# Attention rows: the inverse sums of grouped-query rows move to GpSimd, the high parts of the values to ScalarE

## The chip, the core and the metric

The kernel runs on one core of one Trainium2 chip. The metric is the device time of one execution in microseconds (us), the median of three runs. Five engines work from queues of their own, each strictly in order: TensorE (PE; its weight loads are listed as PEld), VectorE (DVE), ScalarE (ACT), GpSimd (POOL) and SyncE (SP), which issues all DMAs here.

## The reference, cut to what matters

One layer of a diffusion backbone over 2048 latent tokens and 256 context tokens, width 1024. After a modulated RMS norm, one wide projection feeds three parallel mixers (pooling, differential attention, grouped-query attention), each multiplied by a gate path; they are merged and projected out. The change touches the two attentions:

```
def _diff_core(q, k, v, lam):
    s = jnp.einsum('bqhcd,bkhcd->bhcqk', q, k).astype(jnp.float32) * (DIFF_HEAD_DIM ** -0.5)
    p = jax.nn.softmax(s, axis=-1)
    a = (p[:, :, 0] - lam * p[:, :, 1]).astype(v.dtype)
    return jnp.einsum('bhqk,bkhe->bqhe', a, v)

def _gqa_core(q, k, v):
    s = jnp.einsum('bqgrd,bkgd->bgrqk', q, k).astype(jnp.float32) * (GQA_HEAD_DIM ** -0.5)
    p = jax.nn.softmax(s, axis=-1).astype(v.dtype)
    return jnp.einsum('bgrqk,bkgd->bqgrd', p, v)
```

Each of 128 queries by 2304 keys is one *row* below: 4 differential heads with two softmaxes each, 8 grouped-query heads over 2 key/value heads, 16 blocks of 128 queries. That makes 128 differential and 128 grouped-query rows.

## The kernel before

Products keep float32-like accuracy by splitting operands into a high and a low float16 part. There are three stages: projections (to about 565 us of the span), attention (565 to about 2370 us), merge and output projection (to the end).

**A turn of the attention loop.** The loop runs over 256 rows in a fixed order that repeats every four: two differential rows of one query block (called d0 and d1 here), then two grouped-query rows (g0 and g1). Turn i does this for row i (`score_row`, L804 to L822):

- PE: ten matmuls into two PSUM tiles, `sa` (1024 columns) and `sb` (1280 columns). Both have one buffer, so the scores of a row can start only when ScalarE has read the `sa` of the row before.
- DVE: the maximum of `sa` (L815), of `sb` (L816), and the scaled maximum (L817).
- ACT: exponentials of `sa` (L820) and `sb` (L821) into `pt`, each with its sum into column 2 or 3 of the small tile `nm`.

The normalisation lags behind. Two turns later ACT writes `hi`, the float16 of `pt` times the inverse sum (L898, L874), and DVE writes `lo`, the remainder (L903, L879). For a differential row DVE first combines the two softmaxes (L870). SP transposes `hi` and `lo` by DMA into `th`, from which PE forms the products with the values. PE fills the rest of a turn with these products (L917, L943) and with *gate units*, matmuls of another projection that hang on nothing in the attention. So PE always has work beside the scores, but its order is fixed: if the scores wait, what stands behind them waits too.

**Where the inverse sum stands.** `inverse_sum` is two DVE instructions of one column each: add the two sums and scale (L825), reciprocal (L827). For a grouped-query row it is issued first in the turn in which `hi` is made, ahead of the maxima of that turn's row on DVE.

**Where the values are split.** When a head begins, its values are loaded in six parts (`vr`) and split into high and low (`vt`) over three turns, two parts per turn (`load_values`, L787 to L802): a multiply (L798) and a multiply-subtract (L800) for each part, all on DVE, behind L817 of the turn and ahead of its `lo` or combine. There are six such heads (four differential, 128 columns a part of 3 tiles; two grouped-query, 64 columns), so 36 parts in 18 turns.

**Order.** Each engine executes in the order in which the program is written. GpSimd in this stage splits the weight columns of the gate units (`col_split`: L159, L163, L165, twice each for a column, some 36 columns) and squares the differential outputs (L927).

The lines that decide the rest:

```
        for i in range(NR + 7):
            ...
            todo, split_later = split_later, []
            for f in ahead.pop(i, ()):
                f()
            ...
            if i < NR:
                kind, h, j, o, c = rows[i]
                ...
            for f in todo + after.pop(i, []):
                f()
```

`ahead` holds `hi`, `todo` the value splits, `after` the combine and `lo`.

Of the kernel before, what the change touches and what calls it, by code (L numbers as in the profile page):

```python
# [12 lines left out]
F32 = mybir.dt.float32  # L13
F32R = mybir.dt.float32r
I32 = mybir.dt.int32
AF = mybir.ActivationFunctionType
ALU = mybir.AluOpType
# [4 lines left out]
P = 128  # L22
# [10 lines left out]
PSC = 4096.0  # L33
# [24 lines left out]
def block_kernel(ctx: ExitStack, tc, x, xT, ctxt, cc, ada_w, ada_bT, norm_gT, w_qkv, w_gate, gains,  # L58
                 rope_row, rope_col, lam, sublnT, pool_w, pool_scaleT, pool_edge, w_br, w_out, out,
                 dbg=None, stop=9):  # L60
    nc = tc.nc
# [28 lines left out]
    vscale = cst.tile([P, 2], F32, name="vscale")  # L90
# [121 lines left out]
    with tc.tile_pool(name="p1", bufs=1) as sp, tc.tile_pool(name="p1s", bufs=1, space=PSUM) as pp:  # L212
# [460 lines left out]
        for n, kind in enumerate(QKV_ORDER):  # L673
# [12 lines left out]
            for t in range(first, NT):  # L686
                u = t - first
                g, i = divmod(t, 3)
# [67 lines left out]
    with tc.tile_pool(name="p2", bufs=1) as sp, tc.tile_pool(name="p2s", bufs=1, space=PSUM) as pp:  # L756
# [4 lines left out]
        for n in range(32):  # L761
            for o in range(2):
                rows += [("d", n // 8, n % 8, o, c) for c in range(2)]
                m = 2 * n + o
                rows += [("g", m // 8, m % 8, p, 0) for p in range(2)]
        NR = len(rows)
        ahead = {}
# [3 lines left out]
        def at(table, slot, f):  # L771
            table.setdefault(max(slot, 0), []).append(f)
# [10 lines left out]
                    in_=qD[pair][:, half * 64:(half + 1) * 64, j * 256:(j + 1) * 256].rearrange("s p t -> p s t"))  # L783

        VC = 3

        def load_values(key, src, c0, n, m, part):  # L787

            if part == 0:

                use_up((key[0], key[1] - 1))
                values[key] = sp.tile([P, NKT, 2, n], F16, name="vt", tag="vt" + key[0], bufs=1 if key[0] == "d" else 2)
            vt = values[key][:, part * VC:(part + 1) * VC]
            vr = sp.tile([P, VC, n], F32, name="vr", tag="vr", bufs=2)
            dma(out=vr, in_=src[part * VC:(part + 1) * VC, :, c0:c0 + n].rearrange("k p d -> p k d"))

            def split():
                nc.vector.tensor_scalar(out=vt[:, :, 0, :], in0=vr, scalar1=vscale[:, m:m + 1], scalar2=None,  # L798
                                        op0=ALU.mult)
                nc.vector.scalar_tensor_tensor(out=vt[:, :, 1, :], in0=vr, scalar=vscale[:, m:m + 1],  # L800
                                               in1=vt[:, :, 0, :], op0=ALU.mult, op1=ALU.subtract)
            return split  # L802

        def score_row(i, qt, kt, o, m):  # L804

            sa = pp.tile([P, SA], F32, name="sa", tag="sa", bufs=1)
            sb = pp.tile([P, SB], F32, name="sb", tag="sb", bufs=1)
            for k0 in range(0, NTOK, 512):
                k1 = min(k0 + 512, NTOK)
                dst = sa[:, k0:k1] if k0 < SA else sb[:, k0 - SA:k1 - SA]  # L810
                for s in range(2):
                    nc.tensor.matmul(dst, lhsT=qt[:, s, o * P:(o + 1) * P], rhs=kt[:, k0:k1], start=(s == 0),  # L812
                                     stop=(s == 1))
            nm = sp.tile([P, 4], F32, name="nm", tag="nm", bufs=8)
            nc.vector.tensor_reduce(out=nm[:, 0:1], in_=sa, axis=AX.X, op=ALU.max, negate=True)  # L815
            nc.vector.tensor_reduce(out=nm[:, 1:2], in_=sb, axis=AX.X, op=ALU.max, negate=True)  # L816
            nc.vector.tensor_scalar(out=nm[:, 0:1], in0=nm[:, 0:1], scalar1=nm[:, 1:2], scalar2=escale[:, m:m + 1],  # L817
                                    op0=ALU.min, op1=ALU.mult)
            pt = sp.tile([P, NTOK], F32, name="pt", tag="pt", bufs=4)
            nc.scalar.activation(out=pt[:, :SA], in_=sa, func=AF.Exp, scale=escale[:, m:m + 1], bias=nm[:, 0:1], accum_out=nm[:, 2:3])  # L820
            nc.scalar.activation(out=pt[:, SA:], in_=sb, func=AF.Exp, scale=escale[:, m:m + 1], bias=nm[:, 0:1], accum_out=nm[:, 3:4])  # L821
            return pt, nm  # L822

        def inverse_sum(nm, scale):
            nc.vector.tensor_scalar(out=nm[:, 2:3], in0=nm[:, 2:3], scalar1=nm[:, 3:4], scalar2=scale, op0=ALU.add,  # L825
                                    op1=ALU.mult)
            nc.vector.reciprocal(out=nm[:, 3:4], in_=nm[:, 2:3])  # L827

        def part(name):
            return sp.tile([P, NTOK], F16, name=name, tag="parts", bufs=4)  # L830
# [6 lines left out]
        def use_up(key):  # L837
            while any(k == key for k, _ in avs):
                finish_first()

        def turn(src, step, a, o):
            if o == 0:
                while a == 0 and len(live) == 2:

                    finish_first()
                if a == 0:
                    live.append(step)
                turned.setdefault(step, []).append(sp.tile([P, NKT, 256], F16, name="th", tag="turned", bufs=4))
            nc.sync.dma_start_transpose(out=turned[step][a][:, :, o * P:(o + 1) * P], in_=src)
# [3 lines left out]
        def diff_row(i, h, j, o, c):  # L853
            pt, nm = score_row(i, queries[h, j, c], keys[h, c], o, 0)
            if c == 0:
                first[0] = pt, nm
                at(ahead, i + 1, lambda: inverse_sum(nm, lscale[:, 0:1]))
                return
# [4 lines left out]
            def ratio():  # L863

                inverse_sum(nm, lscale[:, 0:1])
                nc.vector.tensor_scalar(out=nm[:, 2:3], in0=nm[:, 3:4], scalar1=n0[:, 2:3], scalar2=neglam[:, 0:1],
                                        op0=ALU.mult, op1=ALU.mult)
# [22 lines left out]
        def gqa_row(i, h, j, o):  # L890
            pt, nm = score_row(i, queries[4 + h, j, 0], keys["g", h // 4], o, 1)
            step = (4 + h, j)
            box = {}

            def high():
                inverse_sum(nm, 1.0 / PSC)
                box["hi"] = part("hi")
                nc.scalar.activation(out=box["hi"], in_=pt, func=AF.Copy, scale=nm[:, 3:4])  # L898
                turn(box["hi"], step, 0, o)

            def low():
                lo = part("lo")
                nc.vector.scalar_tensor_tensor(out=lo, in0=pt, scalar=nm[:, 3:4], in1=box["hi"], op0=ALU.mult,  # L903
                                               op1=ALU.subtract)
                turn(lo, step, 1, o)

            at(ahead, i + 2, high)
            at(after, i + 2, low)
            if o == 1:
                at(fills, i + 4, lambda: (("g", h // 4), gqa_av(h, j, values["g", h // 4], turned.pop(step))))  # L910
# [27 lines left out]
        def gqa_av(h, j, vt, pts):  # L938
            ps = acc("av")
            n = 0  # L940
            for a in range(2):
                for k in range(NKT):
                    nc.tensor.matmul(ps[:, :256], lhsT=vt[:, k, :, :].rearrange("p a d -> p (a d)"),  # L943
                                     rhs=pts[a][:, k, :], start=(n == 0), stop=(n == 2 * NKT - 1))
                    n += 1
                    yield 0.107
            live.remove((4 + h, j))
            r0 = (h % 2) * 64
            ot = sp.tile([P, 256], F32, name="ot", tag="ot", bufs=2)
            sh = sp.tile([64, 256], F32, name="sh", tag="o2", bufs=2)  # L950
            nc.scalar.activation(out=sh, in_=ps[64:128, :256], func=AF.Copy, scale=oscale[64:128, 1:2])
            nc.vector.scalar_tensor_tensor(out=ot[r0:r0 + 64, :], in0=ps[0:64, :256], scalar=oscale[0:64, 1:2], in1=sh,
                                           op0=ALU.mult, op1=ALU.add)
            dma(out=oD[4 + h // 2][r0:r0 + 64, j * 256:(j + 1) * 256], in_=ot[r0:r0 + 64, :])
# [40 lines left out]
        for i in range(NR + 7):  # L995
            row_now[0] = i
            on_act[0] = i >= NR - 2
            avs += [f() for f in fills.pop(i, ())]
            todo, split_later = split_later, []
            for f in ahead.pop(i, ()):  # L1000
                f()
            if i == 0:
                run_gates(HEAD_UNITS - 2)
            if i < NR:
                kind, h, j, o, c = rows[i]
                if kind == "d":
                    diff_row(i, h, j, o, c)
                else:
                    gqa_row(i, h, j, o)
                spent[0] += 1.95  # L1010
            for f in todo + after.pop(i, []):
                f()
            goal = total * (i + 1) / NR if i < NR else spent[0] + 24 * 0.2135 * (i < NR + 4)
            while avs and spent[0] < goal:
                t = next(avs[0][1], None)
                if t is None:
                    avs.pop(0)
                else:
                    spent[0] += t
            while spent[0] < goal:  # L1020
                t = next(dense, None)
                if t is None:
                    break
                spent[0] += t
# [321 lines left out]
```

## Time and profile before

| | |
|---|---|
| median of 3 runs | 2906.23 us (2905.7 to 2908.32) |
| the profiled execution | 2909.97 us, of which span 2908.2 us |
| PE busy | 2787.0 us (96%) |
| DVE busy | 2222.6 us (76%) |
| ACT busy | 1623.7 us (56%) |
| POOL busy | 699.2 us (24%) |

PE is busy nearly throughout, so the profile is read by PE's idle time: where it stands, and what ended it. The shares of the other engines say little by themselves; in the attention stage DVE's is far above its mean. The mean granted TensorE clock is 0.987 of full speed, and 1.00 in most of the attention stage.

### The profile page before, as it was taken

Reading aid. Unit: us, or ns where it says so; the run is one execution under the profiler, and the core shown is the slowest. Engines: PE = TensorE matmul, PEld = TensorE weight load, DVE = VectorE, ACT = ScalarE, POOL = GpSimd, SP = SyncE. Lnnn points to the kernel's source line nnn. Section 1 sums busy time; section 2 is a strip of 40 time slices with the busy share of each in tenths; the row PEclk is TensorE's granted clock in tenths of the full one; section 3 lists DMA queues with packets and bytes.
Section 4 is the critical chain, followed back from the end, with each engine's and each line's share of the span. In section 5 each row is a group of like instructions: output and inputs, shape, how many; then the busy total and the mean of one; then the engine's idle time right before and its main releaser. Section 6 shows DMA issues by size and latency. Waiting matters only on the chain. (4 is left out here: it accounts for less than half of the span.)

```text
span 2908.2 us, 41087 instructions
## 1 busy us (share of the span) xinstructions
PE 2787.0 (96%) x15031; PEld 1653.7 (57%) x15031; DVE 2222.6 (76%) x2829; ACT 1623.7 (56%) x2168; POOL 699.2 (24%) x699
## 2 busy tenths in 40 slices
PE   7999999999999999999989999999999997999999
PEld 2544435655555555555545555555555555787787
DVE  4547657498888898888889888899988856756753
ACT  3844432266766666767756777676776743222221
POOL 1035645411111112110212011202111114443431
PEclk8999999999999999999999999999999998999999
DMA  7345552378888888889798998998987977767674
GB/s 255 109 124 158 138 161 60 104 167 174 184 168 169 178 182 174 167 178 183 161 198 183 180 184 180 176 195 182 185 180 169 184 144 245 238 224 256 208 247 154
DMA packets 1134266, 516.46 MB, mean 178 GB/s; under 512 B 985040, under 2 KB 1038704, under 8 KB 1134064
## 3 DMA queue, kind: packets, MB, share of 16 engines
q1 hardware_dynamic: 1134064, 513.84, 75.2%
q8 instruction: 118, 1.93, 0.3%
q14 instruction: 84, 0.69, 0.1%
HBM read 208.24 MB, written 78.97 MB: 99 GB/s over the span
## 5 line engine op out<-in xcount | busy, mean ns | idle before, releaser
L179 PE MATMUL gate<-hT,gws 128*128 128x512 f16 x3840 | 869.2, 380 | 0.5 <-ACT gt L185 0.5
L179 PEld LDWEIGHTS <-gws 128*128 128x128 f16 x3840 | 373.4, 98 | 419.2 <-issue 17.8
L820 ACT ACTIVATE pt<-sa,nm,escale 128x1024 f32<-128x1024 f32 x256 | 308.3, 1204 | 448.4 <-DVE nm L817 400.2
L812 PEld LDWEIGHTS <-qt 128*128 128x128 f16 x2560 | 249.9, 98 | 356.9 <-issue 72.7
L532 PE MATMUL qkv<-wt,hT 128*128 128x512 f16 (+1 forms) x1920 | 397.3, 362 | 0.0
L816 DVE TENSOR_REDUCE nm<-sb 128x1 f32<-128x1280 f32 x256 | 379.1, 1481 | 0.6 <-PE sb L812 0.6
L815 DVE TENSOR_REDUCE nm<-sa 128x1 f32<-128x1024 f32 x256 | 311.4, 1216 | 71.3 <-PE sa L812 62.2
L821 ACT ACTIVATE pt<-sb,nm,escale 128x1280 f32<-128x1280 f32 x256 | 360.3, 1407 | 0.0
L903 DVE SCALAR_TENSOR_TENSOR lo<-pt,nm,hi 128x2304 f16<-128x2304 f32 x128 | 338.5, 2645 | 6.4 <-ACT hi L898 4.7
L812 PE MATMUL sb<-kt,qt 128*128 128x512 f16 (+1 forms) x1536 | 319.5, 344 | 20.4 <-ACT pt L821 19.3
L898 ACT ACTIVATE hi<-pt,nm 128x2304 f16<-128x2304 f32 x128 | 283.3, 2213 | 95.6 <-issue 44.8
L532 PEld LDWEIGHTS <-hT 128*128 128x128 f16 x1920 | 189.7, 99 | 176.8 <-issue 11.3
L812 PE MATMUL sa<-kt,qt 128*128 128x512 f16 x1024 | 263.0, 379 | 21.7 <-ACT pt L820 17.3
L943 PE MATMUL av<-th,vt 128*128 128x256 f16 x2304 | 266.0, 274 | 13.9 <-DMA th<-hi 7.4
L1190 PE MATMUL br<-bt,wt 128*128 128x512 f32 x1152 | 267.7, 393 | 1.6 <-DVE wt L1045 1.6
L943 PEld LDWEIGHTS <-vt 128*128 128x128 f16 x2304 | 226.2, 98 | 44.7 <-issue 12.8
L1190 PEld LDWEIGHTS br<-bt,wt 128*128 128x128 f32 x1152 | 217.3, 189 | 50.6 <-DVE wt L1045 2.7
L927 POOL TENSOR_TENSOR o<-ot 128x256 f32<-128x256 f32 x32 | 19.7, 614 | 861.4 <-ACT ot L923 861.4
L163 POOL TENSOR_SCALAR gws<-gw 128x512 f16<-128x512 f32 x74 | 68.2, 922 | 597.7 <-PE gate L179 593.8
L917 PE MATMUL av<-th,vt 128*128 128x256 f16 x1728 | 198.9, 273 | 0.0
L1222 PE MATMUL out<-y,wt 128*128 128x512 f32 x768 | 185.0, 399 | 11.6 <-DVE wt L1045 4.9
L917 PEld LDWEIGHTS <-vt 128*128 128x128 f16 x1728 | 169.0, 98 | 19.9
(207 smaller groups left out, 3156.3 us busy)
## 6 DMA issues: line engine op xcount, KB each, us to landing
tD<-gt SPq DMA_DIRECT2D x96, 256.0 KB
wr<-in_w_br SPq DMA_DIRECT2D x32, 768.0 KB
ld<-tD SPq DMA_DIRECT2D x96, 256.0 KB
scan<-in_w_gate SPq DMA_DIRECT2D x40, 512.0 KB
gw<-in_w_gate SPq DMA_DIRECT2D x80, 256.0 KB
qt<-qD SPq DMA_DIRECT2D x256, 64.0 KB
wr<-in_w_out SPq DMA_DIRECT2D x32, 512.0 KB
sgD<-gt SPq DMA_DIRECT2D x48, 256.0 KB
```

Source lines behind the costliest of these rows:

```text
L179: nc.tensor.matmul(ps, lhsT=w[:, b, k, :], rhs=hT[k][:, a, c * CH:(c + 1) * CH], start=(n == 0), stop=(n == 3 * KT - 1))
L532: nc.tensor.matmul(ps[:, :width], lhsT=tokens_of(t, k, a), rhs=wt[k][:, b, :width], start=(n == 0), stop=(n == 3 * KT - 1))
L812: nc.tensor.matmul(dst, lhsT=qt[:, s, o * P:(o + 1) * P], rhs=kt[:, k0:k1], start=(s == 0), stop=(s == 1))
L815: nc.vector.tensor_reduce(out=nm[:, 0:1], in_=sa, axis=AX.X, op=ALU.max, negate=True)
L816: nc.vector.tensor_reduce(out=nm[:, 1:2], in_=sb, axis=AX.X, op=ALU.max, negate=True)
L820: nc.scalar.activation(out=pt[:, :SA], in_=sa, func=AF.Exp, scale=escale[:, m:m + 1], bias=nm[:, 0:1], accum_out=nm[:, 2:3])
L821: nc.scalar.activation(out=pt[:, SA:], in_=sb, func=AF.Exp, scale=escale[:, m:m + 1], bias=nm[:, 0:1], accum_out=nm[:, 3:4])
L898: nc.scalar.activation(out=box["hi"], in_=pt, func=AF.Copy, scale=nm[:, 3:4])
L903: nc.vector.scalar_tensor_tensor(out=lo, in0=pt, scalar=nm[:, 3:4], in1=box["hi"], op0=ALU.mult, op1=ALU.subtract)
L917: nc.tensor.matmul(ps[:, :256], lhsT=vt[:, k, v, :], rhs=pts[a][:, k, :], start=(n == 0), stop=(n == 3 * NKT - 1))
L943: nc.tensor.matmul(ps[:, :256], lhsT=vt[:, k, :, :].rearrange("p a d -> p (a d)"), rhs=pts[a][:, k, :], start=(n == 0), stop=(n == 2 * NKT ...
L1190: nc.tensor.matmul(ps, lhsT=wb[:, a, 4 * br + k, :], rhs=branch_tile(c, br, k)[:, b], start=(m == 0), stop=(m == 11))
```

## The change

Three edits in the attention stage.

1. The values' high part is made by an ACT activation (copy with a scale) in place of a DVE multiply. The low part stays on DVE and reads the high part.
2. For grouped-query rows the two one-column instructions go to GpSimd: add and scale, and a power with exponent -1 in place of the reciprocal. For differential rows they stay on DVE.
3. These two are issued one turn after the row, ahead of the scores of that turn, not in the turn in which `hi` uses them.

```
+        mone = sp.tile([P, 1], F32, name="mone")
+        nc.vector.memset(mone, -1.0)
...
             def split():
-                nc.vector.tensor_scalar(out=vt[:, :, 0, :], in0=vr, scalar1=vscale[:, m:m + 1], scalar2=None,
-                                        op0=ALU.mult)
+                nc.scalar.activation(out=vt[:, :, 0, :], in_=vr, func=AF.Copy, scale=vscale[:, m:m + 1])
                 nc.vector.scalar_tensor_tensor(out=vt[:, :, 1, :], in0=vr, scalar=vscale[:, m:m + 1],
                                                in1=vt[:, :, 0, :], op0=ALU.mult, op1=ALU.subtract)
...
+        def inverse_beside(nm):
+
+            nc.gpsimd.tensor_scalar(out=nm[:, 2:3], in0=nm[:, 2:3], scalar1=nm[:, 3:4], scalar2=1.0 / PSC, op0=ALU.add,
+                                    op1=ALU.mult)
+            nc.gpsimd.tensor_tensor(out=nm[:, 3:4], in0=nm[:, 2:3], in1=mone, op=ALU.pow)
...
             def high():
-                inverse_sum(nm, 1.0 / PSC)
                 box["hi"] = part("hi")
                 nc.scalar.activation(out=box["hi"], in_=pt, func=AF.Copy, scale=nm[:, 3:4])
                 turn(box["hi"], step, 0, o)
...
+            at(ahead, i + 1, lambda: inverse_beside(nm))
             at(ahead, i + 2, high)
             at(after, i + 2, low)
```

The lines of the changed kernel lie up to seven further down: L815 becomes L816, L821 becomes L822, L903 becomes L909, and so on.

VectorE before, at the second of the three turns in which the second differential head's values are split (`vr` are the loaded values, `vt` the split ones, `nm` the small tile of maxima and sums):

```order
L825 TENSOR_SCALAR nm<-nm 128x1
L827 RECIPROCAL nm<-nm 128x1
L825 TENSOR_SCALAR nm<-nm,lscale 128x1
L827 RECIPROCAL nm<-nm 128x1
L815 TENSOR_REDUCE nm<-sa 128x1
L816 TENSOR_REDUCE nm<-sb 128x1
L817 TENSOR_SCALAR nm<-nm,escale 128x1
L798 TENSOR_SCALAR vt<-vr,vscale 128x3x128
L800 SCALAR_TENSOR_TENSOR vt<-vr,vscale,vt 128x3x128
L798 TENSOR_SCALAR vt<-vr,vscale 128x3x128
L800 SCALAR_TENSOR_TENSOR vt<-vr,vscale,vt 128x3x128
L903 SCALAR_TENSOR_TENSOR lo<-pt,nm,hi 128x2304
```

The same place on VectorE in the changed kernel:

```order
L826 TENSOR_SCALAR nm<-nm,lscale 128x1
L828 RECIPROCAL nm<-nm 128x1
L816 TENSOR_REDUCE nm<-sa 128x1
L817 TENSOR_REDUCE nm<-sb 128x1
L818 TENSOR_SCALAR nm<-nm,escale 128x1
L801 SCALAR_TENSOR_TENSOR vt<-vr,vscale,vt 128x3x128 x2
L909 SCALAR_TENSOR_TENSOR lo<-pt,nm,hi 128x2304
```

The first inverse sum and the two multiplies are gone; the two multiply-subtracts stand directly behind the scaled maximum.

ScalarE in the changed kernel, the same turn (the exponentials of `sa` and `sb`, then the two copies, then a gate unit's eviction):

```order
L904 ACTIVATE hi<-pt,nm 128x2304
L821 ACTIVATE pt,nm<-sa,nm,escale 128x1024
L822 ACTIVATE pt,nm<-sb,nm,escale 128x1280
L800 ACTIVATE vt<-vr,vscale 128x3x128 x2
L188 ACTIVATE gt<-gate,ginv 128x512
```

Before, the eviction stood directly behind the two exponentials; the two copies have come between them.

GpSimd in the changed kernel, from the end of one column split to the start of the next (`gw` and `gws` are a weight column, `o_6436` is a squared output):

```order
L165 TENSOR_TENSOR gws<-gw,gws 128x512 x2
L832 TENSOR_SCALAR nm<-nm 128x1
L834 TENSOR_TENSOR nm<-nm,mone 128x1
L832 TENSOR_SCALAR nm<-nm 128x1
L834 TENSOR_TENSOR nm<-nm,mone 128x1
L934 TENSOR_TENSOR o_6436<-ot 128x256
L159 TENSOR_SCALAR gw<-gw,gws 128x512
```

Before, L927 (now L934) followed directly on L165. Now the inverse sums of two grouped-query rows stand between them, behind the whole column split.

## Rows read from the trace of the kernel before

**Rows 1.** Busy time by stretch of the attention stage: stretch, length, engines, clock, DMA.
```profile
564.00:632.00 68.00, 63.61 (x311) 30.53 (x310) 60.57 (x80) 40.69 (x51) 8.78 (x10) 0.97 0.78 176
632.00:1054.00 422.00, 406.33 (x2380) 230.66 (x2379) 369.85 (x412) 287.01 (x344) 66.81 (x63) 1.00 0.84 171
1054.00:1090.00 36.00, 30.37 (x158) 15.21 (x157) 34.22 (x44) 21.29 (x26) 0.00 (x0) 1.00 0.94 204
1090.00:1320.00 230.00, 221.90 (x1285) 124.58 (x1284) 202.89 (x232) 158.31 (x192) 41.15 (x34) 1.00 0.86 173
...
1486.00:1552.00 66.00, 58.18 (x333) 32.11 (x332) 60.26 (x81) 39.82 (x50) 13.75 (x12) 1.00 0.94 191
...
1952.00:1989.00 37.00, 33.20 (x172) 16.61 (x171) 35.55 (x46) 23.94 (x31) 4.45 (x5) 1.00 0.93 190
1989.00:2355.00 366.00, 363.13 (x2147) 208.39 (x2146) 322.11 (x351) 260.29 (x316) 53.92 (x53) 1.00 0.88 176
```

**Rows 2.** Waits, 565 to 2355 us: who waited for whom, total, times, longest.
```profile
ACT pt L820 <- DVE nm L817: 400.2, 213, 9.4
...
PE sb L812 <- ACT pt L821: 19.3, 57, 0.4
PE sa L812 <- ACT pt L820: 17.3, 29, 2.1
```

**Rows 3.** Groups by line: shapes, count, busy us, mean ns, idle before.
```profile
L825 DVE TENSOR_SCALAR nm<-nm 128x1 f32<-128x1 f32 x128 | 26.4, 206 | 1.0
L827 DVE RECIPROCAL nm<-nm 128x1 f32<-128x1 f32 x256 | 42.0, 164 | 8.8
L800 DVE SCALAR_TENSOR_TENSOR vt<-vr,vscale,vt 128x384 f16<-128x384 f32 (+1 forms) x36 | 21.5, 598 | 1.3
L336 ACT ACTIVATE hT<-hf 128x384 f16<-128x384 f32 x40 | 20.9, 523 | 1.3
L798 DVE TENSOR_SCALAR vt<-vr,vscale 128x384 f16<-128x384 f32 (+1 forms) x36 | 19.4, 539 | 3.6 <-DMA vr<-gvD 3.3 <-DMA vr<-vD 0.4
```

**Rows 4.** Timeline of one turn that splits values: start us, duration us, instruction.
```profile
1073.60 0.27 DVE L817 TENSOR_SCALAR nm<-nm,escale 128x1 f32<-128x1 f32 x1
1073.79 0.60 DVE L798 TENSOR_SCALAR vt<-vr,vscale 128x384 f16<-128x384 f32 x1
1073.99 1.20 ACT L820 ACTIVATE pt<-sa,nm,escale 128x1024 f32<-128x1024 f32 x1 [6.18 <-DVE nm L817]
...
1075.19 1.41 ACT L821 ACTIVATE pt<-sb,nm,escale 128x1280 f32<-128x1280 f32 x1
1075.34 1.02 PE L812 MATMUL sa<-kt,qt 128*128 128x512 f16 x4 [2.06 <-ACT pt L820]
...
1075.61 0.62 DVE L800 SCALAR_TENSOR_TENSOR vt<-vr,vscale,vt 128x384 f16<-128x384 f32 x1
...
1076.14 2.61 DVE L870 SCALAR_TENSOR_TENSOR pt<-pt,nm 128x2304 f32<-128x2304 f32 x1
1076.49 0.20 ACT L821 ACTIVATION_READ_ACCUMULATOR pt<-sb,nm,escale 128x1 f32 x1
```

**Rows 5.** Waits, 1486 to 1552 us.
```profile
DVE vt L798 <- DMA vr<-gvD: 3.3, 2, 1.8
```

**Rows 6.** Powers on GpSimd, by line: count, min/median/max ns, first and last start, forms.
```profile
L368 POOL TENSOR_TENSOR r<-s,mhalf x68: 695/1635/1638, 172.8 to 542.1; 128x8 f32<-128x8 f32 x50, 128x2 f32<-128x2 f32 x18
...
L963 POOL TENSOR_TENSOR rr<-rr,mhalf x4: 2910/5214/5258, 1124.3 to 2386.3; 128x16 f32<-128x16 f32 x4
```

**Rows 7.** Timeline: a column split on GpSimd and the next use of an inverse.
```profile
1044.63 0.69 POOL L159 TENSOR_SCALAR gw<-gw,gws 128x512 f32<-128x512 f32 x1
...
1047.37 4.58 POOL L165 TENSOR_TENSOR gws<-gw,gws 128x512 f16<-128x512 f32 x2
...
1052.45 2.22 ACT L898 ACTIVATE hi<-pt,nm 128x2304 f16<-128x2304 f32 x1 [1.04 <-issue]
...
1055.29 1.21 ACT L820 ACTIVATE pt<-sa,nm,escale 128x1024 f32<-128x1024 f32 x1 [0.62 <-DVE nm L817]
```

**Rows 8.** Timeline: a power on GpSimd beside a remainder on VectorE.
```profile
1124.15 2.61 DVE L903 SCALAR_TENSOR_TENSOR lo<-pt,nm,hi 128x2304 f16<-128x2304 f32 x1
...
1124.32 5.26 POOL L963 TENSOR_TENSOR rr<-rr,mhalf 128x16 f32<-128x16 f32 x1 [17.24 <-DVE rr L962]
```

More of the change, by code (lines that the diff above doesn't have):

```diff
@@ L785, in block_kernel @@
         VC = 3
+        mone = sp.tile([P, 1], F32, name="mone")
+        nc.vector.memset(mone, -1.0)
         def load_values(key, src, c0, n, m, part):
@@ L797, in split @@
             def split():
-                nc.vector.tensor_scalar(out=vt[:, :, 0, :], in0=vr, scalar1=vscale[:, m:m + 1], scalar2=None,
-                                        op0=ALU.mult)
+                nc.scalar.activation(out=vt[:, :, 0, :], in_=vr, func=AF.Copy, scale=vscale[:, m:m + 1])
                 nc.vector.scalar_tensor_tensor(out=vt[:, :, 1, :], in0=vr, scalar=vscale[:, m:m + 1],
@@ L827, in inverse_sum, with inverse_beside @@
             nc.vector.reciprocal(out=nm[:, 3:4], in_=nm[:, 2:3])
+        def inverse_beside(nm):
+            nc.gpsimd.tensor_scalar(out=nm[:, 2:3], in0=nm[:, 2:3], scalar1=nm[:, 3:4], scalar2=1.0 / PSC, op0=ALU.add,
+                                    op1=ALU.mult)
+            nc.gpsimd.tensor_tensor(out=nm[:, 3:4], in0=nm[:, 2:3], in1=mone, op=ALU.pow)
         def part(name):
@@ L895, in high @@
             def high():
-                inverse_sum(nm, 1.0 / PSC)
                 box["hi"] = part("hi")
@@ L905, in low @@
                 turn(lo, step, 1, o)
+            at(ahead, i + 1, lambda: inverse_beside(nm))
             at(ahead, i + 2, high)
```

## The prediction

> **What bounds the kernel now.** I read the busy times by stretch first, then the waits, then the timeline of single turns. By stretch, PE has 3 us idle in the last 366 us of the attention stage [rows 1]: there nothing beside PE can gain anything. It idles 15.7 us of 422 and 8.1 us of 230 in the two long stretches between 632 and 1320 us, in which gate units also need DVE. In the four short stretches where a head's values are split it idles 4.4, 5.6, 7.8 and 3.8 us, while DVE is 89, 95, 91 and 96% busy [rows 1]. So DVE sets the pace there, and almost sets it from 632 to 1320 us.
>
> The waits name the link. ScalarE waits 400 us for the scaled maximum (L817), 213 times; PE waits 17.3 and 19.3 us for the exponentials to release `sa` and `sb` [rows 2]. The loop runs PE scores, DVE maxima, exponentials, PE scores. What delays DVE ahead of its maxima delays the next scores but one; what frees it there helps only where PE waits. All such waits together, 36.6 us, are the most that a faster DVE could remove.
>
> **Inverse sums to GpSimd.** DVE loses two instructions for each of 128 grouped-query rows: 0.206 + 0.164 = 0.37 us [rows 3], less some 0.04 of overlap between neighbours (L798 starts 0.19 after the 0.27 of L817 began [rows 4]), so 0.33 us, directly ahead of the maxima. From 1989 us on, where PE hardly idles, they are worth nothing, and so in the stretches between which are not listed: those that are hold 48 us of PE's idle time, more than all its waits for exponentials. Between 632 and 1320 us lie 652 us outside the splits; at 7 us a turn (256 turns in about 1800 us) that is 93 rows, 46 of them grouped-query: at most 46 x 0.33 = 15 us, if every saving reaches PE. Only two rows in four carry a saving, and the 57 waits of 256 rows [rows 2] say that PE does not wait at each; if half the savings are lost to DVE's next wait it is 7.6 us. Nothing there separates the two, so I take the middle, 11 us.
>
> On GpSimd a pair is not shown before. A power takes 0.695 us for 2 columns and 1.636 for 8 [rows 6], 0.157 a column, so about 0.54 for one (an estimate; 2.91 for 16 lies on the same line). The add over one column costs at most the 0.69 of L159's 512 columns [rows 7]; I take 0.3, and 0.9 for the pair with its waits. That is 115 us more on an engine that was busy for 0 to 67 us in each stretch listed [rows 1]. What hides it: the pair can run when the row's exponentials are done, and `hi` needs it a whole turn later. The cover is thinnest behind a column split, which holds the GpSimd queue: one ran from 1044.63 to 1051.95, and `hi` started at 1052.45 [rows 7]. With a pair behind it the inverse would be there at 1052.9, 0.4 us late, of which ScalarE's 0.62 us of idle time before the next exponential [rows 7] takes all. Some 36 columns, half of them ahead of a grouped-query row's `hi`: I take 1 us in all, with 0 and 18 (18 times 1 us) as ends.
>
> **High parts of the values to ScalarE.** This removes 36 multiplies from DVE, 19.4 us [rows 3], and adds 36 copies to ScalarE, each some 0.52 us for 384 elements, as L336 takes for that shape [rows 3]. By sums of busy time it is a gain. By order it is not. The subtract behind it reads the copy, and the copy stands behind both exponentials of its turn, which wait for that turn's L817. So DVE, which went from L817 straight into the split, now stands still until ScalarE has done both exponentials and one copy; `lo` or the combine, and the next row's maxima, queue behind the subtract.
>
> The price, on the turn in the trace [rows 4], counted from the start of L817 at 1073.60. Before: two multiplies, two subtracts, combine at 1076.14, so 2.54 us. After: the exponentials end with the read at 1076.49 + 0.20 = 1076.69, 3.09 us; the copy 0.04 + 0.52; start of the first subtract 0.06 later at 3.71; each subtract 0.53 from its start to the next instruction (1075.61 to 1076.14), so combine at 4.78. That is 2.24 us later. For the six turns with 64-column parts: the multiplies there take 0.42 ((19.4 - 24 x 0.60) / 12 [rows 3, 4]), 0.19 less, so the old path is 4 x 0.19 shorter, the new one 2 x 0.19 and some 0.12 for the copy: 2.5 us. In all 12 x 2.24 + 6 x 2.5 = 42 us on DVE's path, in stretches where it is over 89% busy.
>
> What takes some of it back: nine of the 18 turns have lost an inverse sum, 9 x 0.33 = 3 us. DVE's idle time in the four stretches is 7.4, 1.8, 5.7 and 1.5 us, 16.4 in all [rows 1]. If all of it takes up delay, 42 - 3 - 16.4 = 22.5 us are left; if none, 39. Of the third stretch's 5.7, 3.3 are waits for `vr` [rows 5], which pass while ScalarE is at its exponentials; of the first stretch's 7.4 I count 4.7, since its first two turns have no `lo` yet and DVE stands waiting for the exponentials anyway; of the rest, half, 1.6. So 42 - 3 - 9.6 = 29 us: roughly 10, 5, 9 and 5 by stretch. PE cannot fill that time, since its order is fixed, and gets none of it back later, where it has no idle time to give. As a check, a turn in the new loop is 2.9 for the maxima, 4.8 to `lo` or combine and 2.6 for that, some 10 us, against about 7 for PE.
>
> The queue of SP: the next parts' loads wait until the subtracts free `vr`, and the transposes of `hi` and `lo` stand behind them. Both move with the turn, and the value products that need them come two turns later, so I count 0, with up to 2 us a stretch, 8, as the upper end. Gate evictions stand two copies, 1.0 us, later on ScalarE in 18 turns; the PSUM tiles they free have two others, so 0. The added memset is one instruction outside the loop.
>
> On one point a page bears. A power of 16 columns took 2.91 us by itself and 5.2 in the usual case [rows 6]; in one such case it started 0.17 us into a remainder of 2.61 us on DVE [rows 8]. The Trainium skill (SBUF — State Buffer, section "Who interferes with whom") says that a DVE instruction with two SBUF inputs and a GpSimd instruction that reads SBUF exclude each other for the whole instruction, whoever is first; the trace agrees, with 2.3 us longer beside 2.4 us of remainder left. By that rule a pair on GpSimd that becomes ready just as the exponentials end would hold up the first subtract of a splitting turn by 0.9 - 0.56, some 0.35 us; in nine turns that would make the sum 3 us worse. Without it these are 0.
>
> **Sum.** 29 + 1 - 11 = 19 us slower. Against the profiled execution's own 2909.97 us that is 2929; the median of the runs lies 3.7 us under that execution, so 2925 us.
>
> **Rivals.**
> - *The savings nearly cover the splits.* All of DVE's idle time takes up delay (22.5) and every inverse counts (15): 8 us slower, 2914 us, or 2911 if one stretch hides more. For it: DVE's idle time is there. Against: most of it lies behind waits for exponentials that the splits lengthen. 12%.
> - *Faster: the copy costs DVE no wait.* If the subtracts found their copies ready, DVE would be relieved of 42 us in inverses and 19 us in multiplies, and PE's 36.6 us of waits [rows 2] would shrink by half or more: 2906 - 18 = 2888 us. It decides at one point: whether `lo` or the combine of a splitting turn starts no later than 2.5 us after L817. For it: ScalarE is idle before many exponentials [rows 2]. Against: the copy's place in ScalarE's order. 7%.
> - *GpSimd comes late.* Column splits of 7.3 us and over hold inverses so that `hi`, and behind it the exponentials, wait 1 us or more in 18 turns: 18 us on top, 2943 us. For it: the 0.5 us of margin in rows 7. Against: the turn of lead. 10%.
>
> **How the numbers follow.** The forecast has 71%, with its own range from 2914 (22.5 for 29, 15 for 11) to 2938 (39 for 29, 7.6 for 11). Taking in most of the close race and of the late GpSimd, the range is 2908 to 2941. A measurement of this kernel can tell some 0.2%, 6 us, from no change. Slower by more: the forecast and GpSimd late, and a third of the close race, 85%. Within it: two thirds of the close race, 8%. Faster: 7%.
>
> **What would show it.** In the profile of the changed kernel: DVE idle before L801, waiting for ACT L800, some 3.4 us in each of 18 turns (3.71 less the 0.27 of L817); PE's waits for the exponentials up by about 29 us in the four splitting stretches, and its idle time in the two long stretches between 632 and 1320 us down from 23.8 to about 13 us; pairs on GpSimd of about 0.9 us; `hi` of grouped-query rows hardly ever waiting for GpSimd. It would be wrong if L801 found its copy ready, if PE's waits in those stretches grew by less than 15 us, or if `hi` waited for GpSimd in many turns.

## The result, and the profile after

The changed kernel takes 2925.15 us (median of 6 runs, 2923.58 to 2933.87), against 2906.39 us before on the same chip: a ratio of 1.0065, 95% interval 1.0053 to 1.0076. The profiled execution has a span of 2923.7 us against 2908.2.

The sum of busy times moved as the change suggests: DVE went from 2222.6 to 2164.9 us, ACT from 1623.7 to 1635.9 (less than the 18.1 us of the copies, since neighbouring instructions overlap by some 0.1 us and more of them are now neighbours), POOL from 699.2 to 826.8. PE's busy time hardly changed (2787.0 to 2788.4). Over the whole kernel the lost time is PE's idle time, so the stretches come first. These are those of [rows 1], each splitting stretch drawn out to where its work now ends (columns: stretch, length, busy time of PE, PEld, DVE, ACT, POOL, granted clock, DMA share, GB/s):

```profile
562.00:632.00 70.00, 59.95 (x277) 28.12 (x276) 45.52 (x52) 39.74 (x56) 13.65 (x17) 0.93 0.63 153
632.00:1054.00 422.00, 411.42 (x2411) 233.79 (x2410) 368.30 (x361) 290.36 (x351) 93.32 (x124) 1.00 0.86 174
1054.00:1092.00 38.00, 29.89 (x143) 14.78 (x142) 26.68 (x31) 22.95 (x31) 2.24 (x6) 0.91 0.84 180
1092.00:1320.00 228.00, 223.06 (x1295) 125.61 (x1294) 200.73 (x198) 158.39 (x190) 56.86 (x67) 1.00 0.87 176
...
1486.00:1561.00 75.00, 61.30 (x331) 33.13 (x330) 53.10 (x60) 45.37 (x62) 16.98 (x19) 0.95 0.82 172
...
1961.00:2003.00 42.00, 34.88 (x174) 17.27 (x172) 30.56 (x34) 26.55 (x36) 6.01 (x9) 0.96 0.78 169
2003.00:2370.00 367.00, 363.78 (x2143) 208.81 (x2142) 314.57 (x298) 259.43 (x315) 80.09 (x104) 1.00 0.88 176
```

In the splitting stretches PE now idles 10.1, 8.1, 13.7 and 7.1 us. DVE, which was 89 to 96% busy there [rows 1], is 65 to 73% busy: it is not overloaded any more, it waits. In the two long stretches PE's idle time fell from 15.7 and 8.1 us to 10.6 and 4.9.

The waits of the attention stage (560 to 2380 us) name the new link (who waited for whom: total, times, longest):

```profile
ACT pt L821 <- DVE nm L818: 470.9, 207, 9.1
...
DVE vt L801 <- ACT vt L800: 59.3, 18, 3.6
...
PE sa L813 <- ACT pt L821: 35.1, 24, 3.3
...
PE sb L813 <- ACT pt L822: 16.8, 47, 0.4
ACT hi L904 <- POOL nm L834: 12.6, 7, 2.2
```

DVE waits 18 times, once for each splitting turn, 3.3 us each, for a copy on ScalarE: 59.3 us to save 19.4 us of multiplies [rows 3]. PE's waits for the exponentials grew from 36.6 us [rows 2] to 51.9, and the single ones from 2.1 to 3.3 us. One such turn, the counterpart of [rows 4] (start us, duration us, instruction):

```profile
1077.24 0.27 DVE L818 TENSOR_SCALAR nm<-nm,escale 128x1 f32<-128x1 f32 x1
1077.62 1.21 ACT L821 ACTIVATE pt<-sa,nm,escale 128x1024 f32<-128x1024 f32 x1 [6.87 <-DVE nm L818]
...
1078.82 1.41 ACT L822 ACTIVATE pt<-sb,nm,escale 128x1280 f32<-128x1280 f32 x1
...
1080.22 1.11 ACT L800 ACTIVATE vt<-vr,vscale 128x384 f16<-128x384 f32 x2
1080.37 2.29 PE L813 MATMUL sb<-kt,qt 128*128 128x512 f16 x6 [0.38 <-ACT pt L822]
...
1080.42 0.27 POOL L832 TENSOR_SCALAR nm<-nm 128x1 f32<-128x1 f32 x1 [26.03 <-ACT pt L822]
...
1080.77 0.55 POOL L834 TENSOR_TENSOR nm<-nm,mone 128x1 f32<-128x1 f32 x1
1080.86 1.15 DVE L801 SCALAR_TENSOR_TENSOR vt<-vr,vscale,vt 128x384 f16<-128x384 f32 x2 [3.35 <-ACT vt L800]
...
1081.92 2.61 DVE L877 SCALAR_TENSOR_TENSOR pt<-pt,nm 128x2304 f32<-128x2304 f32 x1
```

From the start of the scaled maximum to the combine it is now 4.68 us; it was 2.54 [rows 4].

**Where the time went, row by row.** Both programs run the same 256 rows in the same order, so the start of the same row's first exponential in two profiles shows when time is lost or won. Before, the starts of rows 12, 72 and 108 read:

```profile
654.96 1.20 ACT L820 ACTIVATE pt<-sa,nm,escale 128x1024 f32<-128x1024 f32 x1 [0.63 <-DVE nm L817]
...
1089.26 1.20 ACT L820 ACTIVATE pt<-sa,nm,escale 128x1024 f32<-128x1024 f32 x1 [0.63 <-DVE nm L817]
...
1316.15 1.20 ACT L820 ACTIVATE pt<-sa,nm,escale 128x1024 f32<-128x1024 f32 x1 [0.62 <-DVE nm L817]
```

In the changed kernel the same three:

```profile
662.56 1.21 ACT L821 ACTIVATE pt<-sa,nm,escale 128x1024 f32<-128x1024 f32 x1
...
1094.72 1.20 ACT L821 ACTIVATE pt<-sa,nm,escale 128x1024 f32<-128x1024 f32 x1 [1.20 <-DVE nm L818]
...
1317.52 1.21 ACT L821 ACTIVATE pt<-sa,nm,escale 128x1024 f32<-128x1024 f32 x1 [1.33 <-DVE nm L818]
```

So the changed kernel is 7.6 us late at row 12, 5.5 at row 72 and 1.4 at row 108. The differences at all turning points (us, kernel minus the kernel before, one profiled execution of each; the last two columns are experiments told of below). What stands at row 0 comes from the projections, which the change does not touch:

| row | what lies ahead of it | changed | inverses only | copies only |
|---|---|---|---|---|
| 0 | projections | -2.2 | 0.0 | -6.8 |
| 12 | first splits (6 turns) | 7.6 | -0.3 | 3.4 |
| 68 | gate units that need DVE | 0.4 | -7.5 | 3.3 |
| 72 | second splits (3 turns) | 5.5 | -7.0 | 9.1 |
| 108 | gate units that need DVE | 1.4 | -11.4 | 9.1 |
| 128 | none | 0.7 | -10.5 | 9.7 |
| 136 | third splits (6 turns) | 9.6 | -13.8 | 19.5 |
| 196 | none | 8.6 | -14.8 | 19.5 |
| 200 | fourth splits (3 turns) | 13.6 | -15.4 | 25.1 |
| 252 | none | 15.2 | -16.0 | 25.5 |

In the changed kernel the four splits lose 9.8, 5.1, 8.8 and 5.0 us, 28.7 in all; the two stretches with gate units win 7.2 and 4.1, 11.3 in all (from the unrounded starts). Elsewhere little moves. From row 0 to row 252 that makes 17.4 us.

### The profile page after: what moved, and what is told of

The parts are those of the page before. It is cut to its first block, busy times and chain, and to the rows that moved or that the text cites. A ratio compares the mean times of both kernels' runs of the same rounds, so it can differ in the third digit from the quotient of the medians.

```text
span 2923.7 us, 41174 instructions
## 1 busy us (share of the span) xinstructions
PE 2788.4 (95%) x15031; PEld 1654.1 (57%) x15031; DVE 2164.9 (74%) x2538; ACT 1635.9 (56%) x2204; POOL 826.8 (28%) x955
## 5 line engine op out<-in xcount | busy, mean ns | idle before, releaser
L821 ACT ACTIVATE pt<-sa,nm,escale 128x1024 f32<-128x1024 f32 x256 | 308.5, 1205 | 526.2 <-DVE nm L818 470.9
L816 DVE TENSOR_REDUCE nm<-sa 128x1 f32<-128x1024 f32 x256 | 312.1, 1219 | 80.7 <-PE sa L813 79.0
L822 ACT ACTIVATE pt<-sb,nm,escale 128x1280 f32<-128x1280 f32 x256 | 360.5, 1408 | 0.0
L909 DVE SCALAR_TENSOR_TENSOR lo<-pt,nm,hi 128x2304 f16<-128x2304 f32 x128 | 336.3, 2627 | 9.2 <-ACT hi L904 6.5
L904 ACT ACTIVATE hi<-pt,nm 128x2304 f16<-128x2304 f32 x128 | 283.0, 2211 | 14.2 <-POOL nm L834 12.6
L832 POOL TENSOR_SCALAR nm<-nm 128x1 f32<-128x1 f32 x128 | 41.3, 322 | 624.7 <-ACT pt L822 619.9
L1229 PE MATMUL out<-y,wt 128*128 128x512 f32 x768 | 183.5, 397 | 12.5 <-DVE wt L1052 5.9
L934 POOL TENSOR_TENSOR o<-ot 128x256 f32<-128x256 f32 x32 | 22.0, 688 | 542.1 <-ACT ot L930 542.1
```

Source lines behind the costliest of these rows:

```text
L1229: nc.tensor.matmul(ps, lhsT=wo[:, a, k, :], rhs=ys[c, k // 2][:, k % 2, b, :], start=(m == 0), stop=(m == 3 * KT - 1))
```

## The experiments

Two theories stood against each other for the loss. *Order*: the copies cost because DVE must wait for them behind the exponentials. *Load*: ScalarE's added 18 to 20 us of work, or a PE that runs slower in the broken-up stretches (granted clock 0.91 to 0.96), costs by itself. For the gain: *relief* of DVE, or the *lead* by which ScalarE has its scale earlier.

**Only the inverses** (the values' multiply back on DVE):

```
-                nc.scalar.activation(out=vt[:, :, 0, :], in_=vr, func=AF.Copy, scale=vscale[:, m:m + 1])
+                nc.vector.tensor_scalar(out=vt[:, :, 0, :], in0=vr, scalar1=vscale[:, m:m + 1], scalar2=None,
+                                        op0=ALU.mult)
```

> The changed kernel with the values' high parts back on VectorE: only the inverse sums of grouped-query rows go to GpSimd. By the wait theory (the copies' place behind the exponentials makes the whole loss, and relieving VectorE between 632 and 1320 us makes the gain) this is faster than before: 2906 - 11.6 from the two long stretches - up to 3 in the splitting ones = about 2893 us. A rival by which GpSimd comes late and eats the gain gives 2906 or more.

Measured: 2893.37 us, before on the same chip 2909.88; ratio 0.9939 (0.9925 to 0.9952). This part of the change makes the kernel faster by itself, some 18 us by the ratio. The table shows where: 7.2 us between rows 12 and 68, 4.4 between rows 72 and 108, 3.4 in the third splits, where DVE now has less to do between its waits.

**Only the copies** (the kernel before, with L798 on ScalarE as in the change):

> The kernel before with only the values' high parts moved to ScalarE, inverse sums as before. By the wait theory it loses the 29 us of the changed kernel and the 3 us that inverses gave back in the splitting turns: about 2938 us. If the two parts of the change do not simply add (the one delaying what the other advances), it lies nearer to 2925 us.

Measured: 2938.94 us, ratio 1.0101 (1.0087 to 1.0115), some 29 us slower. Its column is flat but for four steps at the splits, 10.2, 5.8, 9.8 and 5.6 us. The ratios of the two parts alone, -0.61% and +1.01%, add to +0.40%; the change measured +0.65%. With intervals of 0.11 to 0.14% to each side, whether they add exactly stays open. By the row starts, counted from row 0 to row 252, the two parts together make 16.2 us and the change 17.4, so they nearly add.

**The subtracts behind `lo`** (the changed kernel, one swap):

```
-            for f in todo + after.pop(i, []):
+            for f in after.pop(i, []) + todo:
```

> The changed kernel with one swap on VectorE: in a splitting turn lo or the combine runs first and the two subtracts behind it. ScalarE does the same copies at the same place. By the wait theory the copies are done some 0.9 us after lo, so VectorE hardly waits; the path from L817's start to the end of lo and the subtracts is 4.8 us, against 5.1 before the change: about 2890 us (2893 without this gain). By the rival that the 21 us of added ScalarE work, or the lower TensorE clock of those stretches, makes the loss, the time stays near 2925 us.

Measured: 2891.39 us, ratio 0.9938 (0.9926 to 0.9951). ScalarE does the same copies at the same place, and the loss is gone, so its added work is not the cause. The turn that corresponds to the one above, in this kernel (start us, duration us):

```profile
1064.15 0.27 DVE L818 TENSOR_SCALAR nm<-nm,escale 128x1 f32<-128x1 f32 x1
1064.34 2.61 DVE L877 SCALAR_TENSOR_TENSOR pt<-pt,nm 128x2304 f32<-128x2304 f32 x1
...
1067.13 1.11 ACT L800 ACTIVATE vt<-vr,vscale 128x384 f16<-128x384 f32 x2
...
1067.77 1.15 DVE L801 SCALAR_TENSOR_TENSOR vt<-vr,vscale,vt 128x384 f16<-128x384 f32 x2 [0.82 <-ACT vt L800]
```

DVE makes the combine while ScalarE is at its exponentials and waits 0.82 us for the copy, not 3.35. The granted clock from 1054 to 1092 us is 1.00 there too, so this run does not part the order from the clock; the last section does. Against the run with only the inverses it wins nothing that can be told.

**The copies ahead of the exponentials** (the changed kernel; `split` cut in two, its copy issued before `score_row`):

```
+            for f in todo:
+                if isinstance(f, tuple):
+                    f[0]()
...
-            for f in todo + after.pop(i, []):
+            for f in [f[1] if isinstance(f, tuple) else f for f in todo] + after.pop(i, []):
```

> The changed kernel with the two copies of a splitting turn ahead of that turn's exponentials on ScalarE, subtracts where they were. By the wait theory VectorE finds its copies ready and saves 1.06 us a turn, but the copies (1.1 us) push the exponentials by some 0.5 us where ScalarE had 0.6 us idle, and the copy now waits for its load at a place where the exponentials queue behind it: between 2890 and 2905 us. If the copies' ScalarE time itself made the loss, near 2925 us.

Measured: 2887.33 us, ratio 0.9925 (0.9912 to 0.9939), 3 us below the range expected. The price that was named for it is there (who waited for whom: total, times, longest):

```profile
ACT vt L800 <- DMA vr<-vD: 18.2, 8, 6.1
ACT hi L906 <- POOL nm L836: 12.6, 7, 2.2
DVE vt L803 <- ACT vt L800: 12.5, 8, 3.0
ACT vt L800 <- DMA vr<-gvD: 10.7, 5, 5.9
```

ScalarE waits 28.9 us for loads at the head of its queue, yet DVE's wait for copies falls from 59.3 to 12.5 us, and that decides.

**The inverses on DVE, one turn earlier** (the kernel before):

```
             def high():
-                inverse_sum(nm, 1.0 / PSC)
...
+            at(ahead, i + 1, lambda: inverse_sum(nm, 1.0 / PSC))
             at(ahead, i + 2, high)
```

> The kernel before with one move: the inverse sums of grouped-query rows stay on VectorE but stand one turn earlier, ahead of the maxima of that turn. VectorE's load is the same, ScalarE gets its scale a turn earlier, as in the changed kernel. If the gain of 12 to 13 us came from relieving VectorE, this is as slow as before, 2906 to 2910 us (some us slower where the sum of the exponentials of sb is not there yet when VectorE asks). If it came from the earlier scale, about 2895 us.

Measured: 2906.78 us, before 2908.41; ratio 0.999 (0.9981 to 0.9999). No change that matters: PE's waits for the exponentials stay (560 to 2380 us; total, times, longest):

```profile
DVE nm L825 <- ACT pt L821: 42.3, 126, 3.0
...
PE sb L812 <- ACT pt L821: 22.0, 62, 0.4
PE sa L812 <- ACT pt L820: 18.2, 23, 2.7
```

So with the work left on DVE the earlier scale brings nothing on balance. The run does not part the two fully. Before, in the same window, it read:

```profile
ACT hi L898 <- DVE nm L827: 20.2, 16, 2.5
...
DVE nm L825 <- ACT pt L821: 17.2, 46, 3.0
```

With the earlier scale `hi` no longer waits for the reciprocal, but DVE waits 42.3 us for the sums of the exponentials, not 17.2. That the gain is DVE's relief is shown by the last experiment below.

**The inverses on GpSimd, without the lead** (the run with only the inverses, issued in the turn of `hi`):

```
-            at(ahead, i + 1, lambda: inverse_beside(nm))
+            at(ahead, i + 2, lambda: inverse_beside(nm))
```

> The run with only the inverses on GpSimd (2893 us), with the pair issued in the turn of hi and not one turn ahead. GpSimd's own work is the same; only its order against the column splits is not. If the lead is what hides GpSimd, hi now waits behind the column splits more often than 7 times, in up to 30 turns by 2 us or more, and the time is 2900 to 2915 us. If GpSimd's queue is empty enough anyway, 2893 us.

Measured: 2922.86 us, ratio 1.0049 (1.0036 to 1.0061). It is outside the range expected, on the far side: without the turn of lead the move costs more than it brings, 1.1% against the run with it. ScalarE's `hi` now waits for GpSimd 24 times, 76.6 us, and VectorE's `lo` behind it (the whole execution):

```profile
ACT hi L905 <- POOL nm L835: 76.6, 24, 4.3
...
DVE lo L910 <- ACT hi L905: 41.6, 22, 3.4
```

With the lead it was 12.6 us in 7 waits. GpSimd's work is the same in both; what differs is the turn in which a pair is issued, and so what stands ahead of it in GpSimd's queue.

**The first softmax's inverse to GpSimd as well** (the run with the copies first):

```
-                at(ahead, i + 1, lambda: inverse_sum(nm, lscale[:, 0:1]))
+                at(ahead, i + 1, lambda: inverse_beside(nm, lscale[:, 0:1]))
```

> The run with the copies first (2887 us), with the inverse sum of the first softmax of each differential pair moved to GpSimd as well: 64 pairs of instructions of 0.27 + 0.16 us leave VectorE ahead of the maxima of d1. By the relief theory the 23 pairs between 632 and 1320 us give 23 x 0.4 = 9 us at most; PE's waits there have become fewer, so half, about 2882 us. If what is left of the waits no longer hangs on VectorE's small instructions, 2887 us.

Measured: 2882.12 us, before 2908.41; ratio 0.9911 (0.9897 to 0.9924). It hits the relief theory's number, but its interval overlaps that of the run it builds on, so by the times alone the last step is not shown. The row starts show it, in one execution of each: from row 12 to row 68 this run takes 391.0 us and the run it builds on 394.9, from row 72 to row 108 it is 247.2 and 249.5, so 6.1 us less just where gate units need DVE; from row 108 to row 252 the two differ by 0.5 us. The first softmax's inverse was issued one turn after its row before this edit too, so this step relieves DVE without giving any lead. Both runs beat the kernel before and the changed one.

## Why the prediction was right

*The time.* 2925 was forecast, 2925.15 measured. That they agree to a fraction of a us is luck: the six runs lie between 2923.58 and 2933.87, the interval of the ratio allows 15 to 22 us for the change, and the row starts give 17.4 us for the 19 forecast. What held is the mechanism and the size of its two large terms.

*The copies, 29 us.* The row starts give 28.7, by stretch 9.8, 5.1, 8.8 and 5.0 for 10, 5, 9 and 5. The mechanism is shown twice: the copies alone make the loss, and moving either the subtract or the copy in its queue removes it. Inside a turn the terms were close: the copy took 0.60 us (0.52 forecast from a row of the same shape), the subtract began 3.62 us after the scaled maximum (3.71), the combine 4.68 (4.78), and DVE waited 3.3 us in each of 18 turns (3.4). How much of the delay DVE's idle time would take up was in part chosen: 9.6 us of 16.4, in which the 1.6 is half of the second and fourth stretches' 3.3 and the rest of the first and third stretches is not counted. So the last us or two of the agreement are luck as well. One sign came out smaller than forecast: PE's waits for the exponentials in the four stretches grew from 15.7 to 38.1 us, by 22 and not 29. The rest of the lost time shows as PE busy for longer on the same matmuls (last section).

*The inverses, 11 us.* The row starts give 11.3 in the two stretches with gate units, with whatever the late pairs on GpSimd cost there already in it. PE's idle time in the two long stretches was to fall from 23.8 to about 13 us and fell to 15.5; the starts, which need no model of matmul ends, are the better measure. The middle between 7.6 and 15 was a choice, and it held. Alone, the inverses brought some 18 us by the ratio (14 to 22) and 16 by the row starts, where the forecast's terms make 14 with the 3 of the splitting turns.

*GpSimd, 1 us.* A pair is 0.27 + 0.55 us of work and 0.90 us from start to end (1080.42 to 1081.32 above), for 0.9 forecast. But `hi` "hardly ever" waiting was too mild: 7 waits, 12.6 us, each behind a column split and mostly of 2.1 us, not 0.4. Not all of it is loss: in the same seven turns of the kernel before, `hi` stood idle 6.3 us already, so the pairs added 6.3 us, 0.3 to 1.3 a turn (in the turn of [rows 7] 1.57 us for 1.04, near the 0.4 forecast). As forecast, ScalarE's 0.6 us of idle time before the next exponential takes up part, and about 2.5 us are left for the 1 us counted (an estimate from these turns). In one of the five waits of 2.1 to 2.2 us the split's two last instructions run on (start us, duration us; the turn before the change, then in the changed kernel):

```profile
652.12 2.21 ACT L898 ACTIVATE hi<-pt,nm 128x2304 f16<-128x2304 f32 x1 [0.91 <-ACT sh L951]
...
654.70 4.59 POOL L165 TENSOR_TENSOR gws<-gw,gws 128x512 f16<-128x512 f32 x2
...
659.38 0.27 POOL L832 TENSOR_SCALAR nm<-nm 128x1 f32<-128x1 f32 x1
...
659.73 0.55 POOL L834 TENSOR_TENSOR nm<-nm,mone 128x1 f32<-128x1 f32 x1
660.32 2.21 ACT L904 ACTIVATE hi<-pt,nm 128x2304 f16<-128x2304 f32 x1 [2.08 <-POOL nm L834]
```

What these 7 cost PE was not measured by itself. The rival "GpSimd comes late" is what happens without the lead, so the forecast was right to put its weight on that turn, though it gave no price for losing it.

*The page's 3 us.* By the exclusion that the Trainium skill states (SBUF — State Buffer, "Who interferes with whom") a pair on GpSimd would hold up the first subtract. In the splitting turn shown first the power runs from 1080.77 to 1081.32 and the subtracts start at 1080.86; the two of them take 1.15 us as without it, and none of the 36 took over 0.62. For these powers the trace does not agree, and the 3 us rightly stayed out of the sum. For the longer instructions of a column split it does: in the kernel before, the second of two subtracts started 0.12 us into a split's last two instructions and took 1.46 us, where the first took 0.62:

```profile
595.79 0.62 DVE L800 SCALAR_TENSOR_TENSOR vt<-vr,vscale,vt 128x384 f16<-128x384 f32 x1
...
596.85 2.58 POOL L165 TENSOR_TENSOR gws<-gw,gws 128x512 f16<-128x512 f32 x2
...
596.97 1.46 DVE L800 SCALAR_TENSOR_TENSOR vt<-vr,vscale,vt 128x384 f16<-128x384 f32 x1
```

Where between 0.55 us and a column split the difference begins, no run here shows.

*The rival of a copy that costs no wait* named the point that decides, and it came true in another order: with DVE's wait cut to 12.5 us the same edits take 2887 us, for 2888 in the rival. The closeness of the two times proves nothing, since the rival's 18 us was half of PE's waits, a choice.

## What to carry to other kernels

An instruction that is moved to a less busy engine takes its place in that engine's queue: before counting the busy time saved, follow what stands ahead of it there, who reads its result, and what is queued behind that reader. Here 19 us of multiplies left the busiest helper and brought 59 us of waiting; with the copies two places earlier, or their reader one place later, the loss was gone. That the move then gains anything over leaving the multiplies on DVE is not shown (2887.33 and 2891.39 us against 2893.37, with intervals that overlap). A slow engine with a queue of its own can carry small work at little cost, if it gets it a whole turn ahead: with that lead ScalarE waited 12.6 us for it here, without it 76.6.

## What the runs showed of the hardware that was not expected

The granted TensorE clock fell in the splitting stretches: 0.91 from 1054 to 1092 us, where it had been 1.00 [rows 1]. Six score matmuls took 2.29 us at 1080.37, behind waits of 2.08 and 0.38 us. In the run with the subtracts behind `lo`, at a granted clock of 1.00, they took 1.24; the lower of the clock's two levels, 1.2 for 2.4 GHz, would make that 2.48:

```profile
1067.29 1.24 PE L813 MATMUL sb<-kt,qt 128*128 128x512 f16 x6 [0.38 <-ACT pt L822]
```

In the four splits the same matmuls kept PE busy some 11 us longer than before, so only 17.6 of the 28.7 us lost stand as idle time of PE. The lower clock is still not what made the loss. From row 0 to row 12 the run with only the copies had the same granted clock as the kernel before, 0.98, and PE was busy for the same time, yet it lost 10.2 us; the changed kernel, at 0.95, lost 9.8 (the kernel before, only the copies, the changed kernel; columns as above):

```profile
568.00:655.00 87.00, 82.61 (x445) 43.55 (x444) 78.75 (x98) 56.42 (x69) 12.61 (x12) 0.98 0.72 163
...
561.00:658.00 97.00, 82.82 (x444) 43.36 (x443) 70.89 (x85) 61.52 (x80) 12.98 (x14) 0.98 0.64 147
...
566.00:663.00 97.00, 86.95 (x448) 44.76 (x447) 70.21 (x76) 61.47 (x81) 20.28 (x25) 0.95 0.64 148
```

In each of the three, DVE waited less than 2 us for scores of PE in that stretch. So the slower matmuls fill time in which PE would have stood waiting, and no cost of the clock is shown.
